# Moving the activation and work pools of a one-core network kernel by 64 bytes in SBUF

## The chip, the cores and the metric

The program runs on one core of one Trainium2 chip. The time of a run is the device time of that core in microseconds (us). Every number below that is not from the code or from the allocator comes from the runs of the kernel before or from the profile of one execution of it.

## The reference, cut to what matters

256 tokens of width 1024 pass through two blocks of two layers each. Every layer is a mixer (differential attention, neighbourhood attention, a convolution and pooling mixer, a mixture of two causal attentions) followed by a feed-forward part of width 2816; the first block's layers end with a gated embedding. Nearly all of the arithmetic is products of the activations with weight matrices:

```python
qkv = h @ w_qkv                                   # 1024 x 3072, in three of the four mixers
h = h + mix @ w_o                                 # 1024 x 1024
h = h + (silu(hn @ w_gate) * (hn @ w_up)) @ w_down      # 1024 x 2816 twice, 2816 x 1024
h = h + sigmoid(hn @ w_gate_ple) * (p @ w_proj)   # first block only
```

All values are float32, and each weight is used once per run, for all 256 tokens.

## The kernel before

Activations lie with features on the 128 partitions and the 256 tokens along the free axis. A product keeps float32 accuracy by splitting both operands exactly into two float32r parts, high and low, and by adding three products of parts: weight-high times activation-high, weight-high times activation-low, weight-low times activation-high (`mm3`, which calls `mm`; every matmul of the kernel has the line L195 of `mm` in the profile). One such matmul has a stationary operand of 128x128 and streams a moving operand of 128x256, except in the attentions.

The class `Weights` sets the pace of supply. Each chunk of weights, 128 x 1024 float32 (512 KB), is loaded by SyncE into one of five buffers of the pool `stage`; ScalarE copies it to the high part `w_hi` (L88), VectorE subtracts that to get `w_lo` (L89); eight pairs of these lie in the pool `split`. One chunk feeds 24 matmuls. Loads and splits run ahead of TensorE as far as buffers are free.

The order of TensorE's work is the order in which the code issues it. Attention steps are put between the products of other parts by a counter (`tick`), so that TensorE has products to do while VectorE and ScalarE work on a softmax. The products are of these kinds, named by their output tiles:

- `ps_g` (function `pair`, `out_tile`): the stationary operand is a block of `w_hi` or `w_lo`, the moving one a 128x256 slice of `u_hi` or `u_lo`, the split activations of width 1024. `u_hi` and `u_lo` alternate from matmul to matmul and the slice changes every three matmuls.
- `acc` (class `Acc`): eight output tiles are open at once, the stationary operand is a block of weights, and the moving one is the same pair of slices for all eight. In the feed-forward parts it is `m`, the split middle activation; in the mixers' output products it is a slice of a `u_hi`, `u_lo` pair.
- `ps_v` and `pz`: the weights are the moving operand, 256 or 264 columns wide, and blocks of `u_hi`, `u_lo` are stationary.
- `ps_p`: stationary weights, moving `p_part`, the split embedding input.
- `ps_S`, `ps_t`, `ps_V`: scores, transposes and values of the attentions, on work tiles.

SBUF is handed out by tile pools. A pool's area follows the area of the pool opened before it. Within a pool the tiles lie in the order in which their tags were first asked for, each with as many buffers as it asks for, each rounded up to 32 bytes per partition. The pools are opened in the order `const`, `stage`, `split`, `acts` (the `u` pairs), `work` (everything else). The allocator gave the kernel before these places (byte offset in every partition; the last column is the remainder of that offset by 1024; all buffers of one tag have the same remainder but for those of 32 or 64 bytes):

| tile, pool | first offset | bytes x buffers | remainder |
|---|---|---|---|
| stage, `stage` | 32736 | 4096 x 5 | 992 |
| w_hi and w_lo, `split` | 53216, 85984 | 4096 x 8 each | 992 |
| u_hi and u_lo, `acts` | 118752, 135136 | 8192 x 2 each | 992 |
| sc, bias, ssq, sq, q, k, v (with p_part), on, `work` | 151520 to 189408 | 1024 to 8192 | 992 |
| rstd, `work` | 190432 | 32 x 2 | |
| R, `work` | 190496 | 1024 x 2 | 32 |
| qh (also m), ql, kh (also m), kl, dump, `work` | 192544 to 208928 | 512 to 2048 | 32 |
| st, `work` | 209440 | 32 x 4 | |
| a, at, bv, qb, `work` | 209568 to 222880 | 1024 to 2048 | 160 or 672 |
| zf, ft, lf, fc, then fb, `work` | 224928 to 226848 | 64 to 1536 | |

A slice of 256 float32 is 1024 bytes, so every slice of a `u`, `m` or `p_part` tile keeps its tile's remainder. A stationary block of 128 float32 is 512 bytes, so the blocks of a weight chunk have the remainders 992 and 480 in turn.

Of the kernel before, what the change touches and what calls it, by code (L numbers as in the profile page):

```python
# [10 lines left out]
F32 = mybir.dt.float32  # L11
# [7 lines left out]
S = 256  # L19
# [12 lines left out]

# After how many steps of the products around them the parts of an attention are issued.
LAG = {"da": (2, 8, 11, 14), "da_every": 3, "pair": (2, 5, 7), "every": 2}
# [18 lines left out]
class Weights:  # L53
    """The weights in the order in which TensorE takes them: loaded ahead, each split
    exactly into two float32r parts (w = hi + lo). A chunk with a destination is split
    into tiles that it makes."""

# [49 lines left out]
def network(ctx: ExitStack, tc: tile.TileContext, x_t, p_t, cols, b_v, na_bias, t5_bias, w_mats, out):  # L107
    nc = tc.nc

    const = ctx.enter_context(tc.tile_pool(name="const", bufs=1))  # L110
    stage = ctx.enter_context(tc.tile_pool(name="stage", bufs=N_STAGE))
    split = ctx.enter_context(tc.tile_pool(name="split", bufs=N_HI))
    acts = ctx.enter_context(tc.tile_pool(name="acts", bufs=2))
    work = ctx.enter_context(tc.tile_pool(name="work", bufs=2))
    psum = ctx.enter_context(tc.tile_pool(name="psum", bufs=1, space=PSUM))
    pass

# [1 line left out]
    chunks = []  # L119
# [40 lines left out]

# [1 line left out]
    h = const.tile([128, KT, S], F32, name="h")  # L162
# [6 lines left out]

# [1 line left out]
    off = const.tile([128, S], F32, name="off")  # L171
# [16 lines left out]
    causal = off  # L188
# [13 lines left out]

# [1 line left out]
    clock = [0, 0]  # L204
# [20 lines left out]

    # ---- RMSNorm: the gain goes into the next product's operand, the root mean square
    # into its result ----
    class Norm:
        pass

    def stats_bank(n, b, src, final=False):
        """Sums of squares by token; with final, of the features with the final gain."""
        if b == 0:
            sq = work.tile([128, 2, S], F32, tag="ssq", bufs=2, name="ssq")
        else:
            sq = work.tile([128, 2, S], F32, tag="sq", bufs=1, name="sq")
        if final:
            for i in range(2):
                nc.scalar.activation(sq[:, i, :], src[:, i, :], AF.Square, scale=col("norm_final", 2 * b + i))
        else:  # L240
            nc.scalar.activation(sq, src, AF.Square)
        if b == 0:
            setattr(n, "ssq2" if final else "ssq", sq)
        else:
            ssq = n.ssq2 if final else n.ssq
            if b == 3 and hasattr(n, "end"):
                n.end = sq
            else:
                nc.vector.tensor_add(ssq, ssq, sq)  # L249

    def norm_bank(n, b, src, gain):
        """Bank b (two feature tiles) of the next product's operand from src [128, 2, S]."""
        if b == 0:
            n.u = split_act()
        for i in range(2):
            nc.scalar.activation(n.u[0][:, 2 * b + i, :], src[:, i, :], AF.Copy, scale=gain(2 * b + i))
        for i in range(2):
            nc.vector.scalar_tensor_tensor(n.u[1][:, 2 * b + i, :], src[:, i, :], gain(2 * b + i),  # L258
                                           n.u[0][:, 2 * b + i, :].bitcast(F32),
                                           op0=OP.mult, op1=OP.subtract)  # L260

    def mean_square(ps, ssq, end=None):
        """end: the last bank's squares, where ssq is without them."""
        half = work.tile([128, S], F32, tag="on", bufs=2, name="half")
# [7 lines left out]
    def rstd_a(n, eps=1e-6):  # L272
# [3 lines left out]
        if two:  # L276
            mean_square(ps[:, 2:4], n.ssq2)
        st = work.tile([128, 8], F32, tag="rstd", name="rstd")
        n.rstd = st[:, 0:2]
        nc.vector.tensor_scalar(st[:, 2:4], ps[:, 0:2], 1.0 / D, eps, op0=OP.mult, op1=OP.add)  # L280
        nc.gpsimd.tensor_tensor(n.rstd, st[:, 2:4], mhalf, op=OP.pow)  # L281
        if two:
            # the mean square of what the first norm leaves, and both factors together
            nc.vector.tensor_mul(st[:, 4:6], n.rstd, n.rstd)
# [8 lines left out]
    def spread(v):  # L293
        """v [128, 2], by token, as a row on every partition."""
        ps = psum.tile([128, S], F32, tag="m", bufs=2, name="ps_r")
        for t in range(2):
            nc.tensor.transpose(ps[:, t * 128:(t + 1) * 128], v[:, t:t + 1].to_broadcast([128, 128]), ident)
        r = work.tile([128, S], F32, tag="R", name="R")
        nc.scalar.activation(r, ps, AF.Copy)
        return r  # L300
# [10 lines left out]

# [1 line left out]
    def out_tile(o, u, nk=KT, w=None):  # L313
        """One tile of 128 output features: o [128, S] += W-block^T u."""
        hi, lo = W.take(nk * 128) if w is None else w
# [12 lines left out]
    class Acc:  # L328
        """Products with all eight output tiles open, one k-tile after the other."""

# [39 lines left out]

# [1 line left out]
    def transposes(a, skip):  # L372
        """a [128 q, 2, 256 k] -> [128 k, (k-tile, q)] in one bank, without blocks that are zero."""
        w = 384 if skip else 512
# [28 lines left out]
    def softmax_pair(sc, ps, bias, widths):  # L403
        """Rows of exp(s - max) for two row blocks, unnormalized, and 1/sum."""
        st = work.tile([128, 8], F32, tag="st", bufs=4, name="st")
        for i in range(2):
# [9 lines left out]
    def qkv_group(n, g, kind, bv, steps):  # L416
# [32 lines left out]
        if kind == "od" and g == 0:  # L449
            z = work.tile([128, 2, 8], F32, tag="zf", bufs=1, name="zf")  # L450
            pz = [psum.tile([128, 264], F32, tag=f"acc{2 + t}", name="pz") for t in range(2)]
# [41 lines left out]

# [1 line left out]
    lam = const.tile([128, 4], F32, name="lam")  # L495
# [4 lines left out]
    def small_constants():  # L500
        # the differential attention's bias, -2^-(head + 1) |q - k|
        nc.vector.scalar_tensor_tensor(dist, dist, -1.0, dist, op0=OP.mult, op1=OP.max)
# [19 lines left out]

# [1 line left out]
    def da_steps(g, q, k, v, bias, o, emitted):  # L524
        for p in range(2):
# [23 lines left out]
            def values(p=p, box=box):  # L549
                po = att_psum("V")  # L550
                at = box["at"]
                for qt in range(2):
                    for kk in range(2):
                        mm(po[:, qt * 128:(qt + 1) * 128], at[:, kk * 256 + qt * 128:kk * 256 + (qt + 1) * 128],
                           v[:, kk, p * 128:(p + 1) * 128], kk == 0, kk == 1)
                st = work.tile([128, 8], F32, tag="st", bufs=4, name="st2")
                dump = work.tile([128, 128], F32, tag="dump", bufs=1, name="dump")
# [21 lines left out]

# [1 line left out]
    def pair_steps(g, q, k, v, bias_of, is_causal, o, emitted, later):  # L581
# [79 lines left out]

# [1 line left out]
    na_tiles = {}  # L663
# [16 lines left out]

# [1 line left out]
    extra = {}  # L682

    def fox_prepare(z, extra):
        zz = z.rearrange("p a b -> p (a b)")
        t = work.tile([128, 3, 16], F32, tag="ft", bufs=1, name="ft")
        nc.vector.tensor_scalar(t[:, 0, :], zz, -1.0, None, op0=OP.mult)
# [3 lines left out]
        nc.vector.tensor_scalar(t[:, 2, :], zz, 0.0, None, op0=OP.min)  # L691
        lf = work.tile([128, 2, 8], F32, tag="lf", bufs=1, name="lf")
        nc.vector.tensor_sub(lf.rearrange("p a b -> p (a b)"), t[:, 2, :], t[:, 1, :])

        def cum():
# [3 lines left out]
            mm(ps[:, 1, :], tri, lf[:, 1, :], False, True)  # L699
            extra["f"] = work.tile([128, 2, 8], F32, tag="fc", bufs=1, name="fc")  # L700
            nc.vector.tensor_copy(extra["f"], ps)
# [12 lines left out]

# [1 line left out]
    def silu_times(m, g, other):  # L716
# [47 lines left out]

# [1 line left out]
    p_split = {}  # L766
# [29 lines left out]

# [1 line left out]
    n = Norm()  # L798
# [25 lines left out]

    # between the blocks: h becomes its norm; the product that follows starts from h
    # with both gains, and its result takes both root mean squares
    def scale_h():
# [7 lines left out]

    # even mixer
    y = split_act()
# [90 lines left out]

    # the last norm, with tokens on partitions
    hg = work.tile([128, KT, S], F32, tag="bias", name="hg")  # L930
# [34 lines left out]
def _feature_tiles(w, idx=None):  # L965
    """[K, N] -> [N/128, 128, (K/128) * 128]: a block for each tile of output features."""
    k, n = w.shape
# [8 lines left out]
def _qkv(w):  # L976
    """Per group of 256 columns: two tiles of q, two of k, and v's 256 columns in two halves of k."""
    q, k, v = (_feature_tiles(w[:, i * D:(i + 1) * D]) for i in range(2)) and \
# [12 lines left out]
def _per_partition(v):  # L991
    """[..., n * 128] -> [128, ... * n]"""
    return np.asarray(v).reshape(-1, 128).T
# [96 lines left out]
class _Listed:  # L1090
    """Blocks of several widths, read like an array of blocks."""

# [5 lines left out]
```

## Time and profile before

| | |
|---|---|
| median of 3 runs | 1292.86 us (1291.64 to 1293.36) |
| profiled execution, first to last instruction | 1291.7 us |
| TensorE (PE) busy | 1271.1 us, 98%, 10448 matmuls |
| weight loads (PEld) busy | 1242.7 us, 96% |
| VectorE (DVE) busy | 933.6 us, 72% |
| ScalarE (ACT) busy | 696.7 us, 54% |
| GpSimd (POOL) busy | 31.1 us, 2% |
| DMA | 222.46 MB, mean 172 GB/s |

The page gives no time for the profiled execution other than its span; the median of the runs is 1.2 us above that span. Matmuls overlap in the records: the start of one to the start of the next is the pace, and the duration of one is longer than the pace. "Idle before" is the time that the engine stood before the instructions of a group, and the arrow names what released it.

### The profile page before, as it was taken

What the parts mean: (1) busy time and instruction counts of PE and PEld (TensorE: products, weight loads), DVE (VectorE), ACT (ScalarE), POOL (GpSimd) and SP (SyncE); (2) the same over time, 40 slices, a digit from 0 to 9 for tenths busy, and PEclk for the clock granted to TensorE, in tenths of its full rate; (3) what the DMA queues carried; (4) which work ended last, traced back from release to release, by engine and by line L of the source; (5) the groups of instructions that cost most, each with busy time, mean ns of one, the idle gap of its engine ahead of it and who ended that gap; (6) DMA issues with size and microseconds to landing.
All of it is one profiled execution on the core that took longest, in us unless ns stands there. A gap on an engine that the chain in (4) does not pass through costs nothing.

```text
span 1291.7 us, 25713 instructions
## 1 busy us (share of the span) xinstructions
PE 1271.1 (98%) x10448; PEld 1242.7 (96%) x10448; DVE 933.6 (72%) x1708; ACT 696.7 (54%) x1178; POOL 31.1 (2%) x54
## 2 busy tenths in 40 slices
PE   6999999999999999999999999999999999999997
PEld 6999999999999999999999999999999899999997
DVE  7876766666976667666678888777787766877774
ACT  6776544444666554444456455554456555544543
POOL 1011000000010000000000000000000000000000
PEclk9999999999999999999999999999999999999998
DMA  8465556554646536565546375555545333655530
GB/s 291 146 194 171 174 181 190 186 187 149 208 151 184 172 115 198 185 197 181 175 139 202 133 242 180 182 188 186 180 154 191 107 130 124 208 184 180 185 126 34
DMA packets 62936, 222.46 MB, mean 172 GB/s; under 512 B 7265, under 2 KB 7777, under 8 KB 62689
## 3 DMA queue, kind: packets, MB, share of 16 engines
q1 hardware_dynamic: 60768, 214.52, 50.6%
q0 software_dynamic: 1616, 5.77, 1.9%
q8 instruction: 82, 1.34, 0.4%
q10 hardware_dynamic: 432, 0.53, 0.1%
q14 instruction: 38, 0.30, 0.1%
HBM read 219.74 MB, written 1.05 MB: 171 GB/s over the span
## 4 chain that ended last, share of the span: by engine, by line
PE 91%; DVE 3%; issue 3%; DMA 1%; ACT 1%; POOL 1%; POOLq 0%; DVEq 0%; ACTq 0%; SPq 0%
PE ps_g L195 52%; PE acc L195 26%; PE ps_v L195 5%; PE ps_S L195 3%; PE ps_V L195 2%; PE ps_t L381 1%; DVE w_lo L89 1%; PE ps_p L195 1%; POOL rstd L281 1%; PE pz L195 0%; PE ps_ss L195 0%; DVE u_lo L258 0%; DMA stage<-w_ev_out 0%; DVE ssq L249 0%; DVE h L359 0%
## 5 line engine op out<-in xcount | busy, mean ns | idle before, releaser
L88 ACT ACTIVATE w_hi<-stage 128x1024 fp32r<-128x1024 f32 (+2 forms) x413 | 428.7, 1040 | 447.0 <-PE ps_g L195 176.2
L89 DVE TENSOR_TENSOR w_lo<-stage,w_hi 128x1024 fp32r<-128x1024 f32 (+2 forms) x413 | 495.9, 1202 | 218.9 <-ACT w_hi L88 218.0
L195 PE MATMUL ps_g<-u_hi,w_hi 128*128 128x256 f32 x2048 | 585.5, 287 | 7.4 <-ACT w_hi L88 7.1
L195 PE MATMUL ps_g<-u_hi,w_lo 128*128 128x256 f32 x2048 | 581.6, 284 | 1.0 <-DVE w_lo L89 1.0
L195 PE MATMUL ps_g<-u_lo,w_hi 128*128 128x256 f32 x2048 | 582.0, 285 | 0.4 <-DVE u_lo L258 0.4
L195 PEld LDWEIGHTS ps_g<-u_hi,w_hi 128*128 128x128 f32 x2048 | 393.2, 192 | 11.3 <-ACT w_hi L88 7.1
L195 PEld LDWEIGHTS ps_g<-u_hi,w_lo 128*128 128x128 f32 x2048 | 393.4, 192 | 1.5 <-DVE w_lo L89 1.2
L195 PEld LDWEIGHTS ps_g<-u_lo,w_hi 128*128 128x128 f32 x2048 | 393.7, 192 | 1.1 <-DVE u_lo L258 0.6
L195 PE MATMUL acc<-m,w_hi 128*128 128x256 f32 x1408 | 251.5, 280 | 0.0
L195 PEld LDWEIGHTS acc<-m,w_hi 128*128 128x128 f32 x1408 | 215.6, 188 | 0.3 <-DVE m L724 0.2
L195 PE MATMUL acc<-m,w_lo 128*128 128x256 f32 x704 | 196.7, 280 | 0.0
L195 PEld LDWEIGHTS acc<-m,w_lo 128*128 128x128 f32 x704 | 132.6, 188 | 0.0
L195 PE MATMUL acc<-u_hi,w_hi 128*128 128x256 f32 x256 | 73.6, 291 | 0.0
L195 PE MATMUL acc<-u_lo,w_hi 128*128 128x256 f32 x256 | 72.4, 284 | 0.3 <-DVE u_lo L573 0.3
L195 PE MATMUL acc<-u_hi,w_lo 128*128 128x256 f32 x256 | 72.2, 284 | 0.0
L411 ACT ACTIVATE sc<-sc,st 128x256 f32<-128x256 f32 (+1 forms) x96 | 46.0, 482 | 18.6 <-DVE st L409 18.5
L195 PE MATMUL ps_v<-w_hi,u_hi 128*128 128x256 f32 x176 | 52.2, 296 | 0.0
L195 PE MATMUL ps_v<-w_lo,u_hi 128*128 128x256 f32 x176 | 50.3, 286 | 0.0
L195 PE MATMUL ps_v<-w_hi,u_lo 128*128 128x256 f32 x176 | 50.3, 286 | 0.0
L195 PEld LDWEIGHTS acc<-u_hi,w_hi 128*128 128x128 f32 x256 | 48.8, 192 | 1.5 <-issue 0.6
L195 PEld LDWEIGHTS acc<-u_lo,w_hi 128*128 128x128 f32 x256 | 49.1, 192 | 0.5 <-DVE u_lo L573 0.5
L195 PEld LDWEIGHTS acc<-u_hi,w_lo 128*128 128x128 f32 x256 | 49.0, 192 | 0.0
(189 smaller groups left out, 1223.8 us busy)
## 6 DMA issues: line engine op xcount, KB each, us to landing
stage<-w_gu SPq DMA_DIRECT2D x88, 512.0 KB, 3.9
stage<-w_in SPq DMA_DIRECT2D x88, 512.0 KB, 3.4
stage<-w_down SPq DMA_DIRECT2D x44, 512.0 KB, 4.1
stage<-w_out SPq DMA_DIRECT2D x44, 512.0 KB, 3.4
stage<-w_na_qkv SPq DMA_DIRECT2D x24, 512.0 KB, 4.3
stage<-w_da_qkv SPq DMA_DIRECT2D x23, 512.0 KB, 4.4
stage<-w_od_in SPq DMA_DIRECT2D x22, 512.0 KB, 3.9
stage<-w_gate SPq DMA_DIRECT2D x16, 512.0 KB, 3.4
```

What stands on the lines that cost most here:

```text
L88: self.nc.scalar.activation(hi[:, s], t[:, s], AF.Copy)
L89: self.nc.vector.tensor_sub(lo[:, s], t[:, s], hi[:, s].bitcast(F32))
L195: nc.tensor.matmul(o, a, b, start=start, stop=stop, **kw)
L281: nc.gpsimd.tensor_tensor(n.rstd, st[:, 2:4], mhalf, op=OP.pow)
L381: nc.tensor.transpose(ps[:, o:o + 128], a[:, qt, kk * 128:(kk + 1) * 128], ident)
L411: nc.scalar.activation(sc[:, i, :widths[i]], sc[:, i, :widths[i]], AF.Exp, bias=st[:, 2 + i:3 + i], accum_out=st[:, 4 + i:5 + i])
```

## The change

A pool `shift` with one tile of 128 x 16 float32 (64 bytes per partition) is opened between `split` and `acts`, and GpSimd clears that tile once. The tiny tiles `rstd`, `st`, `st2`, `zf`, `ft`, `lf` and `fc` are taken from a new pool `small`, opened after `work`, with the same shapes, tags and numbers of buffers. The other lines of the diff take away comments and docstrings.

```diff
     split = ctx.enter_context(tc.tile_pool(name="split", bufs=N_HI))
+
+    shift = ctx.enter_context(tc.tile_pool(name="shift", bufs=1))
+    gap = shift.tile([128, 16], F32, name="gap")
+    nc.gpsimd.memset(gap, 0.0)
     acts = ctx.enter_context(tc.tile_pool(name="acts", bufs=2))
     work = ctx.enter_context(tc.tile_pool(name="work", bufs=2))
+    small = ctx.enter_context(tc.tile_pool(name="small", bufs=2))
     psum = ctx.enter_context(tc.tile_pool(name="psum", bufs=1, space=PSUM))
...
-        st = work.tile([128, 8], F32, tag="rstd", name="rstd")
+        st = small.tile([128, 8], F32, tag="rstd", name="rstd")
...
-        st = work.tile([128, 8], F32, tag="st", bufs=4, name="st")
+        st = small.tile([128, 8], F32, tag="st", bufs=4, name="st")
...
-            z = work.tile([128, 2, 8], F32, tag="zf", bufs=1, name="zf")
+            z = small.tile([128, 2, 8], F32, tag="zf", bufs=1, name="zf")
...
-        t = work.tile([128, 3, 16], F32, tag="ft", bufs=1, name="ft")
+        t = small.tile([128, 3, 16], F32, tag="ft", bufs=1, name="ft")
...
-        lf = work.tile([128, 2, 8], F32, tag="lf", bufs=1, name="lf")
+        lf = small.tile([128, 2, 8], F32, tag="lf", bufs=1, name="lf")
...
-            extra["f"] = work.tile([128, 2, 8], F32, tag="fc", bufs=1, name="fc")
+            extra["f"] = small.tile([128, 2, 8], F32, tag="fc", bufs=1, name="fc")
```

## Rows read from the trace of the kernel before

**Rows 1.** The page: busy time by engine, and TensorE's granted clock in 40 slices
```profile
PE 1271.1 (98%) x10448; PEld 1242.7 (96%) x10448; DVE 933.6 (72%) x1708; ACT 696.7 (54%) x1178; POOL 31.1 (2%) x54
PEclk9999999999999999999999999999999999999998
```

**Rows 2.** The page: the chain that ended last, share of the span by line
```profile
PE ps_g L195 52%; PE acc L195 26%; PE ps_v L195 5%; PE ps_S L195 3%; PE ps_V L195 2%; PE ps_t L381 1%; DVE w_lo L89 1%; PE ps_p L195 1%; POOL rstd L281 1%; PE pz L195 0%; PE ps_ss L195 0%; DVE u_lo L258 0%; DMA stage<-w_ev_out 0%; DVE ssq L249 0%; DVE h L359 0%
```

**Rows 3.** Waits of TensorE: total us, times, longest us
```profile
PE ps_g L195 <- ACT w_hi L88: 7.1, 1, 7.1
PE ps_r L297 <- POOL rstd L281: 3.4, 4, 2.5
PE ps_r L297 <- DVE rstd L288: 1.3, 1, 1.3
```

**Rows 4.** The chain in order of time: start us, us, what, how many instructions
```profile
49.20 2.88 PE ps_v L195 x24
...
156.58 11.53 PE ps_g L195 x96
168.11 5.66 PE acc L195 x48
...
294.02 17.28 PE ps_g L195 x144
311.31 11.31 PE acc L195 x96
322.61 1.44 PE ps_p L195 x12
...
753.87 21.12 PE acc L195 x176
...
977.68 5.78 PE pz L195 x48
```

**Rows 5.** Groups by shape: busy us, mean ns | idle before, releaser
```profile
L195 PE MATMUL ps_g<-u_hi,w_hi 128*128 128x256 f32 x2048 | 585.5, 287 | 7.4 <-ACT w_hi L88 7.1 <-DVE z_ev L870 0.3
...
L195 PEld LDWEIGHTS ps_g<-u_lo,w_hi 128*128 128x128 f32 x2048 | 393.7, 192 | 1.1 <-DVE u_lo L258 0.6
...
L195 PE MATMUL acc<-m,w_hi 128*128 128x256 f32 x1408 | 251.5, 280 | 0.0
L195 PEld LDWEIGHTS acc<-m,w_hi 128*128 128x128 f32 x1408 | 215.6, 188 | 0.3 <-DVE m L724 0.2
...
L195 PE MATMUL acc<-u_lo,w_hi 128*128 128x256 f32 x256 | 72.4, 284 | 0.3 <-DVE u_lo L573 0.3
...
L195 PE MATMUL ps_v<-w_hi,u_lo 128*128 128x256 f32 x176 | 50.3, 286 | 0.0
...
L249 DVE TENSOR_TENSOR ssq<-ssq,sq 128x512 f32<-128x512 f32 x35 | 24.1, 689 | 1.6 <-ACT sq L241 1.5
...
L195 PE MATMUL ps_p<-p_part,w_hi 128*128 128x256 f32 x64 | 11.9, 283 | 0.0
...
L195 PE MATMUL ps_p<-p_part,w_lo 128*128 128x256 f32 x32 | 9.1, 284 | 0.0
...
L424 DVE TENSOR_TENSOR q_lo<-q,q_hi 128x512 fp32r<-128x512 f32 x12 | 8.2, 686 | 0.0
```

**Rows 6.** Stretches: length; busy of PE, PEld, DVE, ACT, POOL; clock, DMA share, GB/s
```profile
0.00:33.00 33.00, 22.40 (x154) 21.81 (x155) 24.87 (x48) 20.27 (x32) 5.44 (x15) 0.95 0.84 290
...
142.00:322.00 180.00, 180.00 (x1512) 180.00 (x1511) 118.56 (x158) 82.24 (x114) 0.00 (x0) 1.00 0.57 183
...
784.00:964.00 180.00, 180.00 (x1510) 179.71 (x1509) 137.44 (x222) 92.92 (x136) 0.00 (x0) 1.00 0.57 185
```

**Rows 7.** The stretch after the first norm, columns as in the group above
```profile
24.50:28.00 3.50, 3.50 (x19) 3.50 (x18) 2.90 (x4) 3.50 (x5) 0.00 (x0) 0.51 0.61 222
```

**Rows 8.** GpSimd's first instructions in order of time: start us, us
```profile
1.68 0.10 POOL L179 MEMSET mhalf<- 128x2 f32 x1
1.71 0.11 POOL L181 MEMSET zero<- 128x16 f32 x1
```

More of the change, by code (lines that the diff above doesn't have):

```diff
@@ L112, in network @@
     split = ctx.enter_context(tc.tile_pool(name="split", bufs=N_HI))
+    shift = ctx.enter_context(tc.tile_pool(name="shift", bufs=1))
+    gap = shift.tile([128, 16], F32, name="gap")
+    nc.gpsimd.memset(gap, 0.0)
     acts = ctx.enter_context(tc.tile_pool(name="acts", bufs=2))
     work = ctx.enter_context(tc.tile_pool(name="work", bufs=2))
+    small = ctx.enter_context(tc.tile_pool(name="small", bufs=2))
     psum = ctx.enter_context(tc.tile_pool(name="psum", bufs=1, space=PSUM))
-    pass
     chunks = []
@@ L555, in values @@
                            v[:, kk, p * 128:(p + 1) * 128], kk == 0, kk == 1)
-                st = work.tile([128, 8], F32, tag="st", bufs=4, name="st2")
+                st = small.tile([128, 8], F32, tag="st", bufs=4, name="st2")
                 dump = work.tile([128, 128], F32, tag="dump", bufs=1, name="dump")
```

## The prediction

> **What bounds the kernel now.** I read the page's busy times first. TensorE is busy for 98% of the span at the full granted clock in every slice but the last, which the page gives as 8 tenths [rows 1], and the chain of waits is made of its products: `ps_g` 52%, `acc` 26%, `ps_v` 5% [rows 2]. Then its waits: the largest is the 7.1 us before the first weights, and after that there are 3.4 and 1.3 us in all for the root mean square before `ps_r` [rows 3]. So TensorE hardly ever waits, and the time is the number of its matmuls times their pace. The question is whether the pace can change when nothing but addresses changes.
>
> The chain in order of time answers that, since it gives the pace of each kind of product. In the first feed-forward part 144 `ps_g` take 17.28 us, 120.0 ns each, and the 96 `acc` behind them 11.31 us, 117.8 ns each; shorter pieces say the same, 11.53 us for 96 (120.1 ns; 32 such pieces of 11.52 or 11.53 us) and 5.66 us for 48 (117.9 ns; 36 such pieces, 5.65 to 5.70 us) [rows 4]. Shape, precision, line and clock are the same. The 176 `acc` from 753.87 us are the output product of the convolution mixer, whose moving operand is a `u` pair: 21.12 us, 120.0 ns [rows 4]. So it is not the class `Acc` and not the number of open outputs that makes 117.8. `ps_p`, with `p_part` moving, takes 1.44 us for 12, again 120.0 ns [rows 4]. The groups by shape repeat the split in the durations: weight loads of 188 ns with `m` and of 192 ns with `u`, matmuls of 280 and of 283 to 287 [rows 5].
>
> What separates the fast group from the slow ones is the place of its moving operand. In the allocator's table weights, `u` and `p_part` have the remainder 992 (modulo 1024), and `m` has 32: only `m` stands 64 bytes off the weights. `p_part` lies at 184288, near `m` (192544) and far from `u` (118752), and is slow, so it is the remainder and not the region. My reading is that the stream of the moving operand and the load of the next stationary block get in each other's way when their remainders agree, and lose some 2.2 ns.
>
> The Trainium skill speaks against that. Its page "SBUF — State Buffer", section "Who interferes with whom", gives TensorE two independent read ports, one for the moving operand and one for the weight load, and says that it never waits on anyone; by that rule the shift is worth nothing. The 117.8 and 120.0 ns disagree with the rule as far as two reads of TensorE itself go.
>
> **The change, part by part.** *Where things come to lie.* `u_hi` moves to 118816 and all of `acts` by 64 bytes: remainder 32. In `work` the tags ahead of `rstd` move by 64 too (`sc`, `bias`, `ssq`, `sq`, `q`, `k`, `v` with `p_part`, `on`): 32. From `R` on, the 64 bytes of the two `rstd` that have left cancel the shift, so `m` stays where it is. From `a` on the 128 bytes of `st` are missing as well, so `a` goes down by 128, to 209440. The weights stay at 992. After the change `u` and `p_part` stand to the weights as `m` does now: both 32 against 992 and 480.
>
> *`ps_g`, `acc` with `u`, `ps_p`.* There are 3 x 2048 + 3 x 256 + 64 + 32 = 7008 such matmuls [rows 5]. At 120.0 - 117.8 = 2.2 ns each [rows 4] that is 15.4 us. Not all of it arrives. Up to the first norm and in the stretch at 0.51 of the clock behind it [rows 7] TensorE goes by the loads, by POOL's inverse root and by the lower clock. About 130 of the first 154 matmuls [rows 6] fall under that: 0.3 us less. Before the four later waits for the root mean square, a chain of fixed length on DVE and POOL, some 36 filler matmuls finish earlier and only lengthen the wait: 4 x 36 x 2.2 ns = 0.3 us less. That leaves 14.8 us.
>
> *`ps_v`.* Here the weights stream and `u` is stationary, 3 x 176 matmuls at 2.88/24 = 120.0 ns [rows 4, 5]. The distance becomes 64 bytes the other way round, which no row of these shapes shows. Nearest is `pz`, where the weights stream too, in rows of 1056 bytes, so that their remainder goes 992, 0, 32 against the same `u`: 5.78/48 = 120.4 ns for 264 columns [rows 4], of which the 8 more columns are 3.3 ns at 2.4 GHz. The bounds are 2.2 ns gained and 2.2 lost, 1.2 us either way; I take 0, since the streaming operand keeps its place.
>
> *Attention matmuls on moved work tiles* (`ps_S` in plain float32, `ps_t`, `ps_V`): about 340 records in which one operand moves. With 2.2 ns either way that is 0.7 us at most; I take 0.
>
> *DVE and ACT.* A subtraction of 512 columns takes 689 ns with both inputs at 992 (`ssq`) and 686 with one at 992 and one at 32 (`q_lo`) [rows 5]: no dependence on placement of any size that matters. What there is lies beside TensorE. When that runs 1.2% faster, DVE's share goes from 66% (118.56 of 180 us) to 67% in the first feed-forward and from 76% (137.44) to 77% in the third [rows 6]; the loads go from 185 to 188 GB/s, where 290 were moved in the first 33 us [rows 6]. Neither becomes the bound. What is late next is the softmax chain in the attentions, where TensorE has fillers and shows no wait [rows 3].
>
> *The added clear.* Like `zero`, it is 128x16: 0.11 us, started 0.03 us behind the one before it [rows 8]. Queued behind it on POOL are the iotas and clears of the constants, over by about 2 us, while TensorE starts after 7.1 us [rows 3]. Cost 0; without that cover 0.1 us.
>
> Sum: 1291.7 - 14.8 = 1276.9 us of span. The median of the runs stands 1.2 us above the span of the profiled execution, so the time is 1278 us.
>
> **The rivals.** *Placement is not the cause (no change).* Something else that comes with `m` would make its products fast, for example that they are written shortly before use. Then only the clear remains: 1292.9 us. For it: placement is the only cause I offer, and it is a correlation of four kinds of products. Against: `u` in the mixers' output is also fresh, and `p_part` is old; both are at 120.0. The rule of the Trainium skill quoted above would give this time too. Chance 0.03.
>
> *Only `Acc` products can be fast.* All fast rows are of that kind, with one moving tile for eight blocks, while `ps_g` changes its moving address with every matmul. Then 768 x 2.2 ns = 1.7 us go and the time is 1291.2. Against: at the old place both kinds have the same 120.0 ns. Chance 0.03.
>
> *The attentions keep their time.* If the softmax chains set the pace there and the fillers hide it, the 1152 `ps_g` and 576 `acc` of the attention stages (three attentions of 16 `ps_g` tiles and 8 `acc` steps, 24 matmuls each) would give nothing: 1728 x 2.2 ns = 3.8 us less gain, 1281.9 us. For it: short pieces. Against: no wait of TensorE is listed there. Chance 0.06.
>
> *Slower: the new distance is bad for alternating operands.* `ps_g` alternates `u_hi`, `u_lo`, 16 KB apart. If its stream, now 64 bytes off, runs into the weight load one step later, it may lose as much as `m` gains: 6144 x 2.2 ns = 13.5 us more, less the 1.7 of `acc`, 1304.7 us. It decides as soon as `ps_g` takes more than 120.3 ns (0.3 ns x 6144 = 1.8 us). For it: no row shows that distance in an alternating product. Against: `m` alternates too, between its two halves, 1 KB apart, and `ps_p` alternates and shows the same 120.0 as `acc` with `u`, so alternation has no price at the old place. Chance 0.04.
>
> **How the numbers follow.** The forecast has 0.84. Its own range takes the pace with `u` at 117.4 to 118.4 ns (the pieces of `acc` say 117.8 and 117.9), which is 11 to 18 us, less 0.6, with 1.9 us either way for `ps_v` and the attentions and the runs' spread of 0.9 us: 1274 to 1282. The rival on the attentions lies in it; the others together, 0.10, lie outside, so 1274 to 1282.5 leaves out no more than 2 in 10. A measurement here can tell about 0.2% (2.6 us) from no change. Faster by more: 0.84 + 0.06 = 0.90. Within: the first two rivals, 0.06. Slower: 0.04.
>
> **What would show it.** In the profile after, pieces of 96 `ps_g` take 11.3 us in place of 11.53, 12 `ps_p` take 1.41 or 1.42, pieces of 48 `acc` in the feed-forward stay at 5.66, weight loads of `ps_g` come to 188 ns; `ps_v` tells whether it is the distance or the place of the streaming operand that counts. DVE and ACT durations stay. I am wrong if `ps_g` stays at 120 ns, or if it gets fast and the span does not follow, with new waits of TensorE in the list.

## The result and the profile after

The changed kernel takes 1274.77 us, median of 5 runs (1266.52 to 1276.41), against 1292.28 us for the kernel before, run beside it: a ratio of 0.985 [0.983, 0.988]. It is faster, as forecast, but by 17.5 us where 14.8 were worked out. Its runs fall into two groups: four took 1274.70 to 1276.41 us and one 1266.52 us. The profile (span 1264.8 us) is of that one, so the lines below are not of a run at the median.

The page after, busy time by engine and the granted clock, answers to [rows 1]:

```profile
PE 1242.2 (98%) x10448; PEld 1211.8 (96%) x10448; DVE 932.7 (74%) x1708; ACT 697.5 (55%) x1178; POOL 31.6 (2%) x55
PEclk9999999999999999999999999999999999999998
```

The same instructions, one clear more, and TensorE as busy as before. DVE and ACT do the same work in the same time; only their shares rise. TensorE's waits after, answering to [rows 3]:

```profile
PE ps_g L199 <- ACT w_hi L88: 7.0, 1, 7.0
PE ps_r L301 <- POOL rstd L285: 3.4, 4, 2.5
PE ps_r L301 <- DVE rstd L292: 1.3, 1, 1.3
PE ps_g L199 <- ACT u_hi L260: 1.0, 2, 0.8
...
PE ps_S L199 <- ACT k_hi L427: 0.2, 1, 0.2
...
PE acc L199 <- DVE m L728: 0.2, 1, 0.2
```

None of the waits of [rows 3] has gone, and the three others shown here are new, of 1.0, 0.2 and 0.2 us. The whole list comes to 15.2 us, where it came to 14.2 before. The gain is in the pace, then. The chain in order of time, answering to [rows 4] (start us, us, what, how many instructions):

```profile
25.66 5.66 PE ps_v L199 x48
...
147.32 5.44 PE acc L199 x48
152.76 10.88 PE ps_g L199 x96
...
485.22 5.65 PE acc L199 x48
490.88 11.31 PE ps_g L199 x96
...
654.82 1.41 PE ps_p L199 x12
...
737.02 20.27 PE acc L199 x172
...
780.98 10.88 PE ps_g L199 x96
...
797.47 11.31 PE ps_g L199 x96
...
831.29 10.88 PE ps_g L199 x96
```

The feed-forward parts are counted in order of time, two in each block; a piece is one line of the chain. In the second part (the lines at 485 and 491 us) everything is as predicted: 96 `ps_g` in 11.31 us, 117.8 ns each. In the first part (147 and 153 us) the same code with the same addresses runs at 10.88/96 = 113.3 ns, and `acc` with `m`, which has not moved, goes there too. The third part (from 781 us) changes between the two. Of the 32 pieces of 96 `ps_g`, 13 take 10.88 us and 19 take 11.31. `ps_v` has come down with the rest, to 117.9 ns, and so has `acc` with `u`. The groups by shape, answering to [rows 5]:

```profile
L199 PE MATMUL ps_g<-u_hi,w_hi 128*128 128x256 f32 x2048 | 575.6, 282 | 8.5 <-ACT w_hi L88 7.0 <-ACT u_hi L260 1.0 <-DVE z_ev L874 0.2
...
L199 PEld LDWEIGHTS ps_g<-u_lo,w_hi 128*128 128x128 f32 x2048 | 385.1, 188 | 1.3 <-DVE u_lo L262 0.6
...
L253 DVE TENSOR_TENSOR ssq<-ssq,sq 128x512 f32<-128x512 f32 x35 | 24.1, 688 | 1.6 <-ACT sq L245 1.5
...
L428 DVE TENSOR_TENSOR q_lo<-q,q_hi 128x512 fp32r<-128x512 f32 x12 | 8.2, 686 | 0.0
```

The weight loads with `u` take 188 ns in place of 192; DVE's instructions are the same to a nanosecond (`ssq` 688 for 689, `q_lo` 686 on both sides), though the distance between the two inputs of `q_lo` has changed.

By the starts in the trace, 3388 of the products follow one another at 113 or 114 ns and 5975 at 116 to 119. In the trace before, most with `u` were at 119 to 121 and those with `m` at 116 to 119.

### The profile page after: what moved, and what is told of

It reads as the page before. It is cut to its first block, busy times and chain, and to the rows that moved or that the text cites. A ratio compares the mean times of both kernels' runs of the same rounds, so it can differ in the third digit from the quotient of the medians.

```text
span 1264.8 us, 25714 instructions
## 1 busy us (share of the span) xinstructions
PE 1242.2 (98%) x10448; PEld 1211.8 (96%) x10448; DVE 932.7 (74%) x1708; ACT 697.5 (55%) x1178; POOL 31.6 (2%) x55
## 4 chain that ended last, share of the span: by engine, by line
PE 86%; DVE 5%; issue 3%; ACT 3%; DMA 1%; POOL 1%; POOLq 0%; SPq 0%; DVEq 0%; ACTq 0%
PE ps_g L199 49%; PE acc L199 24%; PE ps_v L199 5%; PE ps_S L199 3%; DVE w_lo L89 2%; PE ps_V L199 2%; PE ps_t L385 1%; ACT w_hi L88 1%; ACT u_hi L260 1%; DMA stage<-w_da_qkv 1%; POOL rstd L285 1%; DVE ssq L253 1%; ACT sq L245 0%; PE pz L199 0%; DVE h L363 0%
## 5 line engine op out<-in xcount | busy, mean ns | idle before, releaser
L199 PE MATMUL ps_g<-u_hi,w_hi 128*128 128x256 f32 x2048 | 575.6, 282 | 8.5 <-ACT w_hi L88 7.0
L199 PE MATMUL ps_g<-u_lo,w_hi 128*128 128x256 f32 x2048 | 571.5, 280 | 0.4 <-DVE u_lo L262 0.4
L199 PE MATMUL ps_g<-u_hi,w_lo 128*128 128x256 f32 x2048 | 570.6, 279 | 0.8 <-DVE w_lo L89 0.8
L199 PEld LDWEIGHTS ps_g<-u_hi,w_hi 128*128 128x128 f32 x2048 | 384.8, 188 | 13.0 <-ACT w_hi L88 7.0
L199 PEld LDWEIGHTS ps_g<-u_hi,w_lo 128*128 128x128 f32 x2048 | 385.4, 188 | 1.3 <-DVE w_lo L89 1.0
L199 PEld LDWEIGHTS ps_g<-u_lo,w_hi 128*128 128x128 f32 x2048 | 385.1, 188 | 1.3 <-DVE u_lo L262 0.6
L199 PE MATMUL acc<-m,w_hi 128*128 128x256 f32 x1408 | 248.5, 279 | 0.2 <-DVE m L728 0.2
```

The source lines that it names most:

```text
L199: nc.tensor.matmul(o, a, b, start=start, stop=stop, **kw)
```

## The experiments

All are edits of the changed kernel; each was run on the same chip as the kernel before, whose times beside them are 1292.9 to 1294.1 us. "Distance" is the remainder of the moving operand less that of the weights, modulo 1024.

**Which part of the change, and is it the distance or the place?** One kernel without the gap, one with the gap ahead of the weights, and one with the gap but the tiny tiles where they were.

```diff
-    gap = shift.tile([128, 16], F32, name="gap")      # e1: no gap; e2: these lines
-    nc.gpsimd.memset(gap, 0.0)                        #     ahead of the pool stage
...
-        st = small.tile([128, 8], F32, tag="rstd", name="rstd")   # e9: all seven tiny
+        st = work.tile([128, 8], F32, tag="rstd", name="rstd")    #     tiles back
```

> The tiny tiles are in the pool at the end, but there is no gap: u stays at 992 and m moves from 32 to 992, so everything stands at distance 0 from the weights. Distance theory: ps_g stays at 120.0 ns and acc with m goes from 117.8 to 120.0 ns, 2112 x 2.2 ns = 4.6 us slower than before, 1297 us; no matmul stream at 113.3 ns. Tiny-tile theory (moving them is what helped): about 1275 us. Theory that m is fast because it was just written: as before, 1292 us.

> As the changed kernel, but the gap lies ahead of the staging buffers: weights, u and m all stand at 32, their distance is 0 again. Distance theory: all products at 120.0 ns, 1297 us. Place theory (only where the moving operand lies counts, 32 good, 992 bad): as the changed kernel, 1266 to 1277 us, with streams at 117.8 and 113.3 ns.

> The gap of 64 bytes stays, the tiny tiles go back to where they were: u at distance 64, m at remainder 96, distance 128. Distance theory: ps_g at 117.9 or 113.3 ns, acc with m at a mixed 118.8 ns as with the gap of 128 bytes, and no stream at 113.3 ns survives an m stretch: 1276 to 1282 us, a little slower than the changed kernel. Tiny-tile theory (half of the gain is theirs): above 1283 us.

Without the gap: 1296.7 us, 1.0026 [1.0015, 1.0036] of the kernel before. With the gap ahead of everything: 1296.98 us, 1.003 [1.0018, 1.0042]. Both came out as the distance theory said, slower than before (by 3.5 and 3.8 us, where 4.6 were worked out), because `m` has lost its distance. The chain of the first and then of the second:

```profile
167.26 5.76 PE acc L196 x48
173.02 11.52 PE ps_g L196 x96
```

```profile
167.87 5.76 PE acc L199 x48
173.63 11.52 PE ps_g L199 x96
```

`acc` with `m`, 5.66 us for 48 before [rows 4], is at 5.76, which is 120.0 ns, in both. In the first `m` stands at 992, in the second at 32, where it was fast before: its own place alone does not set the pace, its distance from the weights does. It is the same for `u`, at 32 in the second and slow. The theories of the place and of fresh data fall, and the tiny tiles alone win nothing. With them back in `work` the time is 1279.34 us, 0.9896 [0.9883, 0.991]:

```profile
138.62 8.39 PE ps_g L198 x74
147.01 5.69 PE acc L198 x48
152.70 11.30 PE ps_g L198 x96
...
181.00 5.70 PE acc L198 x48
186.70 11.30 PE ps_g L198 x96
```

`acc` goes to 118.7 ns, since `m` now stands 128 bytes off, and all 32 pieces of 96 `ps_g` are at 117.8. The first feed-forward part begins at 113.4 ns (8.39 us for 74) and loses that pace with the first piece of `acc`. So moving the tiny tiles matters here because it keeps `m` at 64.

Another rival is that the stream of `u` meets not the weight load but the writes into the weights' buffers, which lie at the same remainder. The trace before speaks against it: `ps_g` took 119.9 ns (3661 products) while ScalarE or VectorE wrote `w_hi` or `w_lo` throughout, 119.7 (976) with no such write, and 119.8 (289) with no transfer by DMA under way either. What meets inside TensorE no run shows; the runs show only that the pace depends on the distance.

**How does the pace depend on the distance?** The gap alone is varied, in steps of 32 bytes.

```diff
-    gap = shift.tile([128, 16], F32, name="gap")
+    gap = shift.tile([128, N], F32, name="gap")   # N = 8, 24, 32, 40, 48, 56, 64, 128
```

> The gap is 32 bytes in place of 64: u and m at remainder 0, distance 32 from the weights. Distance theory: some pace other than 120.0 ns for ps_g and acc alike; if half the distance gives half the relief, 119 ns, 1286 us. Alignment theory (it helps when a row starts at a multiple of 64 bytes): faster than the changed kernel, under 1266 us. No effect below 64 bytes: 120.0 ns, 1297 us.

> The gap is 128 bytes: u and m at remainder 96, distance 128. If the clash depends on the distance modulo 128 bytes: 120.0 ns everywhere, 1297 us. If it depends on the distance up to a longer period: as the changed kernel or better, 1277 us or less, with streams of 117.8 and 113.3 ns; a larger share at 113.3 ns would say that more distance makes the faster pace likelier (all of it: about 1237 us).

> Gap of 96 bytes, distance 96 for u and m. So far: distance 0 gives 120.0 ns a matmul, 32 a mixed 116.6 (1273 us), 64 either 113.3 or 117.9 (1266 to 1276 us), 128 a mixed 118.8 (1288 us). If the price falls and rises smoothly between 64 and 128: about 118 ns, 1278 us. If each distance has a rhythm of its own: any mixture between 113 and 122 ns, 1237 to 1300 us.

> Gap of 192 bytes, distance 192. Period of 128 bytes (with distance 128 near 0 and 192 like 64): streams at 117.9 and 113.3 ns, 1266 to 1277 us. Longer period: another mixture, between 113 and 122 ns.

> Gap of 256 bytes, distance 256. If the clash has a period of 256 bytes or a divisor: 120.0 ns everywhere, 1297 us. If its period is 512 or 1024 bytes: another pace.

> Gap of 512 bytes, distance 512, which is the length of one stationary block. Blocks of a chunk stand at 992 and 480 in turn, and at distance 0 both had 120.0 ns, so with any period that divides 512 this is distance 0 again: 120.0 ns, 1297 us. A pace below 119 ns would say that the period is longer.

> Gap of 224 bytes, distance 224, which is 32 bytes short of the period of 256. If the clash is the same for both signs of the distance: as with 32 bytes, a mixed 116.6 ns, 1273 us. If the sign matters: another mixture, between 113 and 122 ns, 1240 to 1300 us.

> Gap of 160 bytes, distance 160, the last multiple of 32 bytes in the period of 256. If the sign of the distance does not matter: like 96 (160 is 96 short of 256), a mixed 120.0 ns, 1297 us. As for 32 against 224 (116.6 and 118.3 ns) the sign does matter: any mixture between 113 and 122 ns, 1240 to 1300 us.

| distance, bytes | 96 `ps_g` in the chain, us | ns each | time, us |
|---|---|---|---|
| 0 (before) | 11.52 or 11.53 | 120.0 | 1292.9 (`m` at 64) |
| 0 (e1, e2) | 11.52 | 120.0 | 1296.7, 1297.0 |
| 32 | 11.20 | 116.7 | 1272.93 |
| 64 (the change) | 11.31 or 10.88 | 117.8 or 113.3 | 1274.77 |
| 96 | 11.52 | 120.0 | 1296.86, one run |
| 128 | 11.39 | 118.6 | 1288.06 |
| 160 | 11.26 or 11.39 | 117.3 or 118.6 | 1282.62, one run |
| 192 | 10.88 or 11.31 | 113.3 or 117.8 | 1253.62, one run; timed again below: 1260.33 |
| 224 | 11.36 | 118.3 | 1283.79, one run |
| 256 | 11.52 | 120.0 | 1297.22, one run |
| 512 | 11.52 | 120.0 | 1295.6, one run |

At 256 and 512 the pace is as at 0, and at 128 it is not: as far as tested, the slow pace of distance 0 comes back after 256 bytes. Within the period the pace does not fall and rise smoothly (96 is as bad as 0), and the sign matters (32 and 224 differ, as do 96 and 160). Several expectations missed: 32 was put at 119 ns, 128 is neither at 120.0 ns nor as good as the change, and 192, which has the two paces of 64, is faster than the range given for that. Distance 32 is as fast as the change, with one pace in nearly all pieces and all four runs within 1.6 us. At 160 there are two paces, 18 pieces at 117.3 ns and then 14 at 118.6. The chains at 32, 96, 128, 160 and 224:

```profile
171.72 11.20 PE ps_g L199 x96
```

```profile
173.92 11.52 PE ps_g L199 x96
```

```profile
174.13 11.39 PE ps_g L199 x96
```

```profile
172.79 11.26 PE ps_g L199 x96
...
824.43 11.39 PE ps_g L199 x96
```

```profile
172.38 11.36 PE ps_g L199 x96
```

The chain at 256, and at 192 in the timed kernel below:

```profile
173.98 11.52 PE ps_g L199 x96
185.50 5.76 PE acc L199 x48
```

```profile
163.86 5.44 PE acc L199 x48
169.30 10.88 PE ps_g L199 x96
```

**Two paces at one distance.** The changed kernel was profiled again, the gap of 192 timed, and a disturbance added to the first block's feed-forward parts.

```diff
             middle(j, ps, n.R, mids[j])
+            if middle is swiglu_mid and j % 4 == 3:     # e14
+                px = psum.tile([128, 4], F32, tag="m", bufs=2, name="ps_x")
+                mm(px[:, 0:1], ident, ones, True, True)
```

> The changed kernel once more, for a second profile. Theory of two states (at distance 64 the stream falls into 113.3 or 117.9 ns after each disturbance and keeps it): 1266 to 1277 us, with other stretches at 113.3 ns than in the first profile, and a span that is longer by 4.5 ns for each matmul that is at 117.9 in place of 113.3. Theory that the place in the program sets the state: the same stretches at 113.3 ns and the same span within 1 us.

> The gap of 192 bytes again, timed: 1250 to 1260 us in every run if distance 192 makes the 113.3 ns stream the likely one; up to 1277 us in some runs if its first look was a lucky one. All at 113.3 ns would be about 1240 us.

> The changed kernel with one added float32 product of one column behind every fourth step of the first block's two feed-forward parts (ten in all; their result is not used). They cost about 0.25 us each, 2.5 us. Theory that a disturbance draws the state anew and undisturbed streams keep it: the streams of some 1540 matmuls in these parts break up, their pace changes between 113.3 and 117.9 ns at the added products, and the runs lie closer together than the two groups of the changed kernel (1266.5 to 1268.9 and 1274.7 to 1276.4). Theory that the state is set by the place in the program: the first feed-forward keeps 113.3 and the second 117.9 ns on both sides of the added products.

The changed kernel again: 1268.86, 1276.18, 1268.25 and 1275.82 us, the same two groups, 0.984 [0.982, 0.987] of before. The second profile has the first feed-forward at 113.3 ns and the second at 117.8, like the first profile, and differs in the third:

```profile
186.59 10.88 PE ps_g L199 x96
...
543.04 11.31 PE ps_g L199 x96
...
799.35 11.31 PE ps_g L199 x96
```

In the first profile the third part changes pace on its way, from 10.88 (at 780.98 us) to 11.31 (at 797.47) and back (at 831.29). So the place alone does not set the pace. The second span is 2.2 us longer: 312 fewer products at 113 or 114 ns would make 1.4 us, and the stretch after the first norm at the lower clock, which only the second profile has (0.59 of the clock, 1.00 in the first), some 1.5.

In each part of the first block one pace holds for some 1540 products; one such stream at 113.3 in place of 117.8 is 6.9 us, about the distance between the two groups of runs (7.5 us). That the first part makes the groups is argued from this; no run of the upper group was profiled. The two profiles of the gap of 192 show a whole part at either pace, in the same program. The second feed-forward part in the first of them (span 1251.8 us) and in the second (1259.3 us):

```profile
484.86 5.44 PE acc L199 x48
490.30 10.88 PE ps_g L199 x96
```

```profile
484.52 5.65 PE acc L199 x48
490.18 11.31 PE ps_g L199 x96
```

That part takes 171.4 us in the one and 178.1 in the other, 6.7 of the 7.4 us between the spans, on two chips at full granted clock.

The disturbed kernel: 1276.45 to 1279.14 us, 2.7 us apart where the changed kernel's runs lie 9.9 apart. Its chain in the first part, with a product added behind every second piece of 96, which cuts it in two:

```profile
170.93 11.31 PE ps_g L199 x96
182.24 5.65 PE acc L199 x48
187.89 5.66 PE ps_g L199 x48
193.66 5.76 PE ps_g L199 x48
```

The last line includes a longer interval of 0.20 us behind an added product. By the starts, the part that ran at 113.3 ns in both profiles of the changed kernel is at 117.8 from end to end. That again speaks against the place in the program, but also against a draw with even odds at each disturbance: after the added products, and also ahead of the first of them, it was always 117.8. The added products need not be the reason: the third part, which has none, is at 117.8 here too, and no run of the changed kernel is on record beside this one on its chip. By the starts an added product costs 0.22 us; without the ten, the median of 1277.7 us would be 1275.5, the time of the changed kernel's upper group, which fits a slow first part there.

What decides between the paces stays open. A stream can keep one for some 1540 products. In the five profiles at 64 and 192 a change from 113.3 to 117.8 ns came, but for one case of 53 (between stretches of at least 24 products), across an interval longer than 130 ns. The way back needs none: in the third part of the first profile the intervals go from 118 to 113 ns at 828.5 us, within a piece of `acc`, without a wait.

The gap of 192 timed: 1260.33 us (1258.71 to 1265.11), 0.9756 [0.9739, 0.9773] of before; the changed kernel beside it had 0.984 [0.982, 0.987], so this beats the change in both its groups. 5263 products ran at 113 or 114 ns in this profile, 7326 in its first, against 3388 and 3076 in the two of the changed kernel. Only one of its five runs lies in the expected 1250 to 1260 us, and the 1253.62 of the first run was not reached again.

## Why the prediction was right in kind and wrong in size

- *The bound and the cause* hold. TensorE's pace is the time, the list of waits is nearly the same (15.2 us for 14.2), and the distance from the weights sets the pace (e1, e2). The four kinds of products in the old trace, sorted by remainder, were enough to find it, and the sentence of the Trainium skill's page "SBUF — State Buffer", section "Who interferes with whom", that TensorE never waits on anyone does not hold for its two reads: 120.0 ns at distances 0, 256 and 512 and 113.3 at 192.
- *The step that failed* is the term of `ps_g`, `acc` and `ps_p`: "7008 x 2.2 ns", with a range of 117.4 to 118.4 ns. I took the pace of `m` in the old trace for the pace of distance 64. There `m` came in pieces of 48 between `ps_g` that ran at 120.0 ns. Once both stand at 64, a second pace of 113.3 ns can last, and a third of the products took it. The kernel with the tiny tiles back bears this out: with `u` at 64 and `m` at 128 the first part began at 113.4 ns and lost it with the first piece of `acc`. That also moved a term I had at zero, `acc` with `m`. The mean pace of `ps_g`, without intervals over 130 ns, went from 119.9 to 116.1 ns in the profile, outside the range that I gave it, and so the time came out just under the lower edge: the ratio 0.9853 is 1273.9 us on the median shown. The edge was also tighter than its own terms, which added in full reach down to 1272.5 us. How much of the gain at the median, a run of the upper group, comes from 113.3 ns stays open, since none of that group was profiled.
- *`ps_v`*, taken at 0 with 2.2 ns either way, gained: 117.9 ns for 120.0, about the upper bound of 1.2 us (1.1 in the second profile, 2.1 in the first with the clock of the first norm). The sign I was unsure of is the distance of 192.
- *The attention's own products, DVE, ACT and the clear*: 0, as costed; `q_lo` is at 686 ns on both sides.
- *The profiled span* fell by 26.9 us. Counted from the start of each product to the start of the next, `ps_g`, `acc` with `u` and `ps_p` became 22.1 us shorter, where 14.8 were forecast, `acc` with `m` 2.8 and `ps_v` 2.1, where 0 was; scores, values and transposes did not change (under 0.1 us each). The first norm's stretch at half the clock [rows 7] is missing in this profile, worth some 1.5 us of that; the second profile of the same kernel has it, so that goes with the run and not with the change. Over the same products, the second part gave 2.2 us, which is the forecast pace, and the first 9.0. The third and fourth gave 5.5 and 2.6. There a part of what the faster pace brings is lost again, since `acc` now catches up with `m`: pieces of 48 at 5.55 to 5.61 us where 5.44 would be undisturbed.
- *The rivals*: no change and only `Acc` fell at once, the attentions kept no time back (the three stretches are 1.8, 1.3 and 1.4 us shorter over the same products), and the slower rival (the alternating operands lose) is refuted by 11.31 and 10.88. None of them was the case that came: I had no rival in which the gain was larger.

## What to carry to other kernels

When one kind of product runs some per cent faster than another of the same shape, compare the addresses of what it reads before looking for a wait: a free experiment may already stand in the trace. For products like these, place moving operands with a chosen distance from the stationary ones modulo 256 bytes, and measure several distances, since the best (192 here) is not the first that helps. A pace read off products that stand between slower ones need not be the pace that they reach without them; leave room for a better one. Where runs fall into groups, profile one of each before explaining the median.

## What the runs showed of the hardware

Products of 128x128 by 128x256 float32r, back to back with a weight load each, ran at 120.0 ns at the distances 0, 256 and 512 between moving and stationary operand, at 116.7 ns at 32, 120.0 at 96, 118.6 at 128, 117.3 or 118.6 at 160, 118.3 at 224, and at 113.3 or 117.8 ns at 64 and 192, all at full granted clock. At 64 and 192 a stream kept one of the two paces for up to some 1540 products. Two runs of one program, with the gap of 192, had spans 7.4 us apart, 6.7 of them in one such part, without a difference in clock.
